# RWKV-7 time mixer on one core: when the triangular solve and the block inverses are done, and which engine forms the keys' factors

## The chip, the cores and the metric

The kernel runs on one core of a Trainium2 chip. Its engines run side by side, each with its own queue in program order: TensorE (PE, matrix products, with PEld for its weight loads), VectorE (DVE), ScalarE (ACT), GpSimd (POOL) and SyncE (SP), which here only issues DMAs. The metric is the time of one launch in microseconds of the device; the median of three runs of the kernel before is 1370.06 us (1367.29 to 1370.53).

## The reference

A two-layer encoder trunk, 512 tokens, 1024 channels, float32. Layer 0 mixes tokens with RWKV-7, layer 1 with latent attention; each layer also has a ConvFFN with gated GELU. The change touches the RWKV-7 mixer alone:

```
def _rwkv7_step(S, inp):
    r, w, k, v, a, b = inp
    sa = einsum('bhvk,bhk->bhv', S, a)
    S = S * w[:, :, None, :] + sa[..., None] * b[:, :, None, :] + v[..., None] * k[:, :, None, :]
    return S, einsum('bhvk,bhk->bhv', S, r)

def rwkv7_time_mix(x, ...):
    xs = x + (x_prev - x) * mu                    # six mixtures
    r, k, v = (xs[i] @ w_rkv[i] for i in range(3))
    w_log = -softplus(-(w0 + tanh(xw @ w1) @ w2)) - 0.5
    decay = exp(-exp(w_log))
    a = sigmoid(a0 + (xa @ a1) @ a2)
    g = sigmoid(xg @ g1) @ g2
    kk = normalize(k * k_k)                       # per head of 64 channels
    k = k * (1.0 + (a - 1.0) * k_a)
    y = scan(_rwkv7_step, zeros, (r, decay, k, v, -kk, kk * a))
    yn = groupnorm(y) * lnx_w + lnx_b
    bonus = sum(r * k * r_k) * v
    return ((yn + bonus) * g) @ w_o
```

## The kernel before, in words

**Tiling.** Channels lie on partitions, in 8 tiles `p` of 128 (two heads each); tokens lie in the free dimension, 512 of them. The recurrence is done in 8 chunks of 64 tokens: within a chunk, the term `a` makes a triangular system of 64 by 64 for each of the 16 heads, which is inverted; across chunks a state `S` of 64 by 64 a head is carried. Matrix products with weights are three passes of a shorter float32 format (`mm3`, L131 to L133); for that each weight tile is split into a high part by ScalarE (`whi`) and a rest by VectorE (`wlo`, L125).

**Stages of `time_mix`.** First the projections, in three groups: keys, values, receptances. While TensorE runs the values' projection, the *key tiles* are formed, interleaved by `keyed`: `factors(p)` makes the decay factors (`ar[..., 0, :]` holds exponentials shifted by one token, `ar[..., 1, :]` unshifted ones, `en` their inverse), `ka` = `a * k_a + (1 - k_a)`, and the squares `ksq`; `key2(p)` sums these on TensorE (`ps_kn`), makes the reciprocal root `krv` and finishes both halves of `ar` and `bk`; `ab(p)` multiplies the two for the triangular systems and writes them to DRAM (`s_ab`) with DMAs that GpSimd issues. `recept(p)` then multiplies the receptances in, takes the decay at each chunk's end (`pc`), and makes `rkk` for the bonus; `bonus(p)` sums that on TensorE (`ps_bo`).

**The solve.** `solve()` is a generator of 2 times 31 steps on VectorE, each two `tensor_tensor` (into `tm`, then onto the matrix, both L85; in the rows the solve's tiles are `s` or `s_1562`). Its first half inverts the 32 by 32 diagonal blocks of chunks 0 to 3, its second half those of chunks 4 to 7. At a half's end GpSimd writes the result out (`s_xd`), ScalarE copies a transposed half, and GpSimd writes that too (`s_x1`). Only then, for the second half, ScalarE copies the next matrix in (`sA`), and a memset and ones are laid down.
`steps(n)` issues n steps at a place of the program: two with each input tile of the receptances' first three output tiles (18), then per tile from the table at L698, then per chunk from the table at the chunk loop.

**The inverses.** `fetch_x(ch)` reads a chunk's blocks back from DRAM (nine kinds of pieces, on SyncE's queue), into `TB[ch % 2]`, `LT` and `X1`. `inv1` (matmuls `ps_i1`, then a copy `wi`) and `inv2` (`ps_i2`, copied into `TB`) complete the 64 by 64 inverses. The kernel before does chunk 0's and chunk 1's before the chunk loop and then, in chunk `ch`, those of `ch + 2`.

**The chunk loop.** A chunk does `u_step` (`ps_u` from `v` and `lu`), half of the next chunk's scores (`ps_sc`, masked by VectorE into `lu` and `m`), `u2_step` (`ps_u` from `TB` and `u`), the other scores, state product (`s_step`), token transposes (`ps_tk`), outputs and the transposes of the chunk before. The output's gates (`gate(p, hf)`: four matmuls of 256 columns for 8 tiles, and for each half of the tokens) lie in chunks 0 and 4: in chunk 0 four tiles ahead of `u2_step` and four at the chunk's end.

**What sets the order.** A list scheduler orders the instructions of each engine, by program order and by offsets of priority: weights are brought forward (by 70, and 160 in `proj`), steps of the solve not (`SP = 0`). What is ready early is put early, so an instruction can stand well before its place in the program, but each engine then runs its queue strictly in that order: an instruction that waits holds all behind it.

Of the kernel before, what the change touches and what calls it, by code (L numbers as in the profile page):

```python
# [48 lines left out]
def c3(ap):  # L49
    return ap.rearrange("q (c t) -> q c t", t=C)  # L50
# [6 lines left out]
class Trunk:  # L57
# [243 lines left out]
    def time_mix(self, nxt, cp, gt):  # L301
# [8 lines left out]
        ap = self.open("apool")  # L310
        ar = ap.tile([P, DT, NCH, 2, C], F32, name="ar")
        bk = ap.tile([P, DT, NCH, 2, C], F32, name="bk")
# [5 lines left out]
        lw = self.open("lw", side="right")  # L318
        scan = t1.tile([P, T], F32, name="scan")
        w1 = lw.tile([P, D], F32, tag="w1", name="w1")  # L320
        g1 = [lw.tile([P, n], F32, tag=f"g{i}", name="g1") for i, n in enumerate((512, 768))]
        g1k = lambda o, n: g1[0][:, o:o + n] if o < 512 else g1[1][:, o - 512:o - 512 + n]
        x = self.x
# [112 lines left out]
        qk = group(1, 0, first, prio=G0)  # L436
        for t, n in ((w1, I["w1"]), (g1[0], I["g1"][:, :512]), (g1[1], I["g1"][:, 512:]), (self.cst, I["cst"][:, :256]), (self.ident, I["cst"][:, 256:]), (scan, I["scan"])):
            nc.sync.dma_start(out=t, in_=n)
# [61 lines left out]
        for p in range(5, DT):  # L500
            kept(p, qk[p - 5])
        nc.gpsimd.memset(ar[:, :, :, 0, 0:1], 1.0)
        self.use_log_exp()

        def factors(p):
            cp = cs[:, p, :]
            self.act(ar[:, p, :, 0, 1:C], c3(cp)[:, :, 0:C - 1], AF.Exp, scale=-CD)
            en = t1.tile([P, T], F32, tag="en", name="en")
            self.act(en, cp, AF.Exp, scale=CD)
            ka = t1.tile([P, T], F32, tag="ka", name="ka")  # L510
            self.act(c3(ka), bk[:, p, :, 0, :], AF.Identity, scale=V("ka", p), bias=om[:, 48 + p:49 + p])
            self.act(ar[:, p, :, 1, :], c3(cp), AF.Exp, scale=-CD)
            self.tt(ka, ka, en, ALU.mult)
            self.tt(bk[:, p, :, 0, :], bk[:, p, :, 0, :], c3(en), ALU.mult)
            kr = tp.tile([P, T], F32, tag="kr", name="kr", bufs=3)
            self.act(c3(kr), bk[:, p, :, 1, :], AF.Copy, scale=V("kk", p))
            sq = tp.tile([P, T], F32, tag="sq", name="ksq", bufs=3)
            self.act(c3(sq), bk[:, p, :, 1, :], AF.Square, scale=V("kk", p))
            self.tt(bk[:, p, :, 1, :], bk[:, p, :, 1, :], c3(ka), ALU.mult)
            return p, kr, sq  # L520

        def key2(p, kr, sq):
            pn = bank2("ps_kn")
            mm(pn, lhsT=self.bones, rhs=sq, start=True, stop=True)
            rv = tp.tile([P, T], F32, tag="sq", name="krv", bufs=3)
            self.act(rv, pn, AF.Ln, bias=self.tiny)
            self.act(rv, rv, AF.Exp, scale=-0.5)
            self.stt(kr, rv, 1e12, kr, ALU.min, ALU.mult)
            self.tt(ar[:, p, :, 0, :], c3(kr), ar[:, p, :, 0, :], ALU.mult)
            self.tt(bk[:, p, :, 0, :], c3(kr), bk[:, p, :, 0, :], ALU.mult)  # L530
# [144 lines left out]
        def recept(p, q):  # L675
            nc.vector.tensor_copy(out=self.pc[:, :, p], in_=ar[:, p, :, 1, C - 1])
            self.tt(ar[:, p, :, 1, :], c3(q), ar[:, p, :, 1, :], ALU.mult)
# [16 lines left out]
        for p in range(DT):  # L694
            q = qr[p] if p < 3 else proj(0, p)
            if len(rp) == BL:
                bonus(*rp.pop(0))
            steps((0, 0, 0, 7, 7, 3, 3, 3)[p])  # L698
            rp.append(recept(p, q))
            if p in (5, 7):  # L700
                fetch_x(p // 2 - 2)
                w = inv1(p // 2 - 2, bank2)
            if p == 6:
                inv2(0, w, bank2)
        def score_mm(ch, g):
# [7 lines left out]
        while rp:  # L713
            bonus(*rp.pop(0))
        inv2(1, w, bank2)
        gate_weights()
# [20 lines left out]
        WU.append(buf("u"))  # L737
        self.sign = s1.tile([P, 1], F32, name="sign")
        nc.vector.tensor_copy(out=self.sign, in_=self.mincl[:, C - 1:C])
        M, LU, VS, S, YC, ends = {}, {}, {}, {}, {}, {}  # L740
# [123 lines left out]
        for ch in range(NCH):  # L864
            n = ch + 1
            u = u_step(ch)
            if n < NCH:
                scores(n, (0,))
            if ch == 0:
                for p in range(4):  # L870
                    gate(p, 0)
            u2_step(ch, u)
            if n + 1 < NCH:
                fetch_x(n + 1)
            if n < NCH:
# [6 lines left out]
            if ch < 3:  # L882
                steps((11, 12, 1)[ch])
            y_tokens(ch, q)
            if ch > 0:
                yt(ch - 1)
            if ch in (0, 4):
                for p in range(0 if ch else 4, DT):
                    gate(p, ch // 4)
            if n + 1 < NCH:  # L890
                fetch_v(n + 1)
                w = inv1(n + 1)
            if 5 <= ch:
                fill(2)
            if n + 1 < NCH:
                inv2(n + 1, w)
            if ch == 6:
# [420 lines left out]
```

## Time and profile before

| | |
|---|---|
| median of three runs | 1370.06 us |
| the profiled execution, its own time | 1370.63 us |
| its span | 1368.9 us |
| granted TensorE clock, mean over the span | 0.975 |
| PE busy | 1307.6 us, 96% (8108 instructions) |
| PEld busy | 1077.8 us, 79% |
| DVE busy | 815.6 us, 60% |
| ACT busy | 708.8 us, 52% |
| POOL busy | 291.8 us, 21% |
| moved by DMA | 141.41 MB, 103 GB/s on average |

The span is that of the recorded instructions; the execution's own time is 1.7 us more. The busy times are sums over the whole program. A granted clock of 1 is TensorE's higher level (2.4 GHz), 0.5 its lower one (1.2 GHz); a number between is a mean over the stretch. In a row of the trace the first number is the start in us from the span's beginning, the second the duration, and a bracket at the end gives the time that the engine stood idle before the row and what released it.

### The profile page before, as it was taken

How to read it: one execution, taken by the hardware profiler on the slowest of the kernel's cores; microseconds unless marked ns; L12 is line 12 of the kernel's file. 1: busy time of each engine (PE TensorE's matmuls, PEld its weight loads, DVE VectorE, ACT ScalarE, POOL GpSimd, SP SyncE). 2: the span in 40 equal slices, each digit the busy share in tenths (PEclk: the TensorE clock that was granted, in tenths of full speed). 3: DMA queues.
4: the chain of work that ended last, by engine and by line, in shares of the span. 5: the costliest groups of instructions: out<-in, count | busy, mean ns of one | idle time of the engine just before them, and what ended most of it. 6: DMA issues, size and time to landing. Idle time of an engine off the chain costs nothing.

```text
span 1368.9 us, 21882 instructions
## 1 busy us (share of the span) xinstructions
PE 1307.6 (96%) x8108; PEld 1077.8 (79%) x8108; DVE 815.6 (60%) x1512; ACT 708.8 (52%) x1353; POOL 291.8 (21%) x277
## 2 busy tenths in 40 slices
PE   7989997989999999999999999999999999999995
PEld 5467775878998888888888877777898888888885
DVE  7668787677797666665233887873566555541003
ACT  6699842567676444444232566674464444433231
POOL 0001421100010000000000241222355444444443
PEclk9999998899999999999999999999999999999998
DMA  6121593345533323223333145441223222233321
GB/s 208 61 77 63 169 260 90 77 106 132 170 124 124 100 94 100 98 95 92 94 98 94 44 119 116 106 106 47 78 77 101 100 93 100 99 90 93 97 77 62
DMA packets 111211, 141.41 MB, mean 103 GB/s; under 512 B 47552, under 2 KB 54592, under 8 KB 111104
## 3 DMA queue, kind: packets, MB, share of 16 engines
q1 hardware_dynamic: 107696, 129.52, 32.2%
q0 software_dynamic: 3408, 10.49, 2.4%
q8 instruction: 64, 1.05, 0.3%
q14 instruction: 43, 0.35, 0.1%
HBM read 120.31 MB, written 12.58 MB: 97 GB/s over the span
## 4 chain that ended last, share of the span: by engine, by line
PE 75%; DVE 11%; ACT 7%; issue 3%; DMA 2%; POOL 1%; SPq 0%; POOLq 0%; ACTq 0%; DVEq 0%
PE ps_in L132 11%; PE ps_in L133 11%; PE ps_in L131 11%; PE ps_out L131 7%; PE ps_out L133 7%; PE ps_out L132 7%; PE ps_pj L132 1%; PE ps_pj L131 1%; PE ps_pj L133 1%; PE ps_o L1185 1%; DVE wlo L125 1%; DVE x L220 1%; PE ps_sc L710 1%; PE ps_t L1169 1%; ACT whi L82 1%
## 5 line engine op out<-in xcount | busy, mean ns | idle before, releaser
L82 ACT ACTIVATE whi<-wraw 128x512 fp32r<-128x512 f32 (+2 forms) x411 | 249.6, 614 | 356.9 <-PE ps_out L133 132.9
L132 PE MATMUL ps_in<-xl,whi 128*128 128x512 f32 (+1 forms) x768 | 286.9, 374 | 4.8 <-DVE xl L88 4.8
L131 PE MATMUL ps_in<-xh,wlo 128*128 128x512 f32 (+1 forms) x768 | 286.8, 374 | 0.8 <-DVE wlo L125 0.7
L125 POOL TENSOR_TENSOR wlo<-wraw,whi 128x512 fp32r<-128x512 f32 (+2 forms) x176 | 221.8, 1266 | 304.4 <-ACT whi L82 299.0
L133 PE MATMUL ps_in<-xh,whi 128*128 128x512 f32 (+1 forms) x768 | 285.7, 373 | 0.0
L125 DVE TENSOR_TENSOR wlo<-wraw,whi 128x512 fp32r<-128x512 f32 x229 | 154.0, 679 | 92.7 <-ACT whi L82 90.8
L132 PEld LDWEIGHTS ps_in<-xl,whi 128*128 128x128 f32 x768 | 145.5, 190 | 31.3 <-DVE xl L88 6.3
L131 PEld LDWEIGHTS ps_in<-xh,wlo 128*128 128x128 f32 x768 | 145.3, 190 | 26.7 <-DVE wlo L125 0.9
L133 PEld LDWEIGHTS ps_in<-xh,whi 128*128 128x128 f32 x768 | 145.6, 190 | 24.8
L131 PE MATMUL ps_out<-hh,wlo 128*128 128x512 f32 (+1 forms) x396 | 146.6, 370 | 1.3 <-ACT mg L82 1.3
L133 PE MATMUL ps_out<-hh,whi 128*128 128x512 f32 (+1 forms) x396 | 145.3, 367 | 0.0
L132 PE MATMUL ps_out<-hl,whi 128*128 128x512 f32 (+1 forms) x396 | 144.1, 364 | 0.0
L85 DVE TENSOR_TENSOR macc<-macc,msq 128x512 f32<-128x512 f32 (+1 forms) x25 | 15.5, 619 | 136.1 <-ACT msq L82 136.1
L237 POOL TENSOR_TENSOR row<-row,msq 128x256 f32<-128x256 f32 x14 | 14.1, 1010 | 379.8 <-ACT msq L82 379.3
L131 PE MATMUL ps_pj<-xh,wlo 128*128 128x512 f32 x192 | 79.0, 430 | 8.6 <-ACT xh L82 6.7
L88 DVE SCALAR_TENSOR_TENSOR c<-gp,vec,c 128x512 f32<-128x512 f32 x88 | 72.6, 827 | 24.1 <-ACT c L82 22.7
L131 PEld LDWEIGHTS ps_out<-hh,wlo 128*128 128x128 f32 x396 | 74.4, 188 | 13.5 <-ACT mg L82 1.9
L133 PEld LDWEIGHTS ps_out<-hh,whi 128*128 128x128 f32 x396 | 74.3, 188 | 13.5
L132 PEld LDWEIGHTS ps_out<-hl,whi 128*128 128x128 f32 x396 | 74.3, 188 | 13.1
L132 PE MATMUL ps_pj<-xl,whi 128*128 128x512 f32 x192 | 77.2, 404 | 0.3 <-DVE xl L85 0.2
L133 PE MATMUL ps_pj<-xh,whi 128*128 128x512 f32 x192 | 76.5, 400 | 0.0
L85 DVE TENSOR_TENSOR u<-ps_in,row 128x512 f32<-128x512 f32 x44 | 30.3, 689 | 63.0 <-PE ps_in L133 63.0
(289 smaller groups left out, 2385.2 us busy)
## 6 DMA issues: line engine op xcount, KB each, us to landing
wraw<-in_win SPq DMA_DIRECT2D x176, 256.0 KB, 2.7
wraw<-in_wout SPq DMA_DIRECT2D x80, 256.0 KB, 2.6
wraw<-in_wrkv SPq DMA_DIRECT2D x48, 256.0 KB, 3.2
wraw<-in_wo SPq DMA_DIRECT2D x32, 256.0 KB, 2.9
x<-in_xT SPq DMA_DIRECT2D x16, 256.0 KB, 4.7
wraw<-in_ow SPq DMA_DIRECT2D x16, 256.0 KB, 3.1
s_ab<-ab POOLq DMA_DIRECT2D x16, 128.0 KB, 2.8
s_vt<-vT POOLq DMA_DIRECT2D x8, 256.0 KB, 2.8
```

Source lines behind the costliest of these rows:

```text
L82: self.nc.scalar.activation(out=out, in_=in_, func=func, **kw)
L85: self.nc.vector.tensor_tensor(out=out, in0=a, in1=b, op=op)
L88: self.nc.vector.scalar_tensor_tensor(out=out, in0=a, scalar=s, in1=b, op0=op0, op1=op1)
L125: self.wlo.tensor_tensor(out=l[:, :w], in0=r, in1=h[:, :w].bitcast(F32), op=ALU.subtract)
L131: mm(ps, lhsT=wl, rhs=xh, start=start, stop=False)
L132: mm(ps, lhsT=wh, rhs=xl, start=False, stop=False)
L133: mm(ps, lhsT=wh, rhs=xh, start=False, stop=stop)
L220: eng.tensor_tensor(out=xk, in0=xk, in1=mg, op=ALU.add)
L237: (self.nc.gpsimd if (h, k) in ACCP else self.nc.vector).tensor_tensor(out=self.acc2[:, c], in0=self.acc2[:, c], in1=sq, op=ALU.add)
L710: mm(qs[hd][:, p], lhsT=b, rhs=a, start=True, stop=True)
L1169: nc.tensor.transpose(out=q[:, o:o + P], in_=pr[i][:, j * P:(j + 1) * P], identity=t.ident)
L1185: nc.tensor.matmul(q[HALF[i], j * P:], lhsT=VT[pr // 4][j][:, c:c + 64], rhs=w, start=j == 0, stop=j == QB - 1)
```

## The change

Key tiles: the shifted exponential (8 of ScalarE's) is dropped. `before(p)` reads the unshifted one with an offset of one token, after a memset of 1.0 on VectorE in the last column of each chunk. For this `ar` becomes a view of a larger tile `art`, and `w1`, `g1` and `scan`, which are used before `ar` is written, are laid into it (with one DMA for `g1` instead of two). The keys' bias form `ka` goes from ScalarE to VectorE, the copy `pc` from VectorE to ScalarE.

Solve and inverses: the solve's steps come after `recept` in the loop over tiles, with the table (0, 0, 0, 5, 5, 4, 0, 0), which is 32 steps ahead of the chunk loop with the 18 of the first three tiles; the rest lies in the chunks. Chunk 0's blocks are fetched after the projections, and its inverse is done among the gates of chunk 0, now all eight of them ahead of `u2_step`. From there on chunk `ch` does the inverse of `ch + 1`. `sign` is a view instead of a copy.

```diff
-        ar = ap.tile([P, DT, NCH, 2, C], F32, name="ar")
+        art = ap.tile([P, DT * NCH * 2 * C + P], F32, name="ar")
+        ar = art[:, :DT * NCH * 2 * C].rearrange("q (p c s t) -> q p c s t", p=DT, c=NCH, s=2)
...
-        nc.gpsimd.memset(ar[:, :, :, 0, 0:1], 1.0)
+        def before(p):
+            nc.vector.memset(ar[:, p, :, 0, C - 1:C], 1.0)
+            o = p * NCH * 2 * C + C - 1
+            return art[:, o:o + NCH * 2 * C].rearrange("q (c s t) -> q c s t", s=2, t=C)[:, :, 0, :]
         def factors(p):
             cp = cs[:, p, :]
-            self.act(ar[:, p, :, 0, 1:C], c3(cp)[:, :, 0:C - 1], AF.Exp, scale=-CD)
...
-            self.act(c3(ka), bk[:, p, :, 0, :], AF.Identity, scale=V("ka", p), bias=om[:, 48 + p:49 + p])
+            nc.vector.tensor_scalar(out=c3(ka), in0=bk[:, p, :, 0, :], scalar1=V("ka", p), scalar2=om[:, 48 + p:49 + p], op0=ALU.mult, op1=ALU.add)
...
-            self.tt(ar[:, p, :, 0, :], c3(kr), ar[:, p, :, 0, :], ALU.mult)
+            self.tt(ar[:, p, :, 0, :], c3(kr), before(p), ALU.mult)
...
         def recept(p, q):
-            nc.vector.tensor_copy(out=self.pc[:, :, p], in_=ar[:, p, :, 1, C - 1])
+            self.act(self.pc[:, :, p], ar[:, p, :, 1, C - 1])
...
-            steps((0, 0, 0, 7, 7, 3, 3, 3)[p])
             rp.append(recept(p, q))
-            if p in (5, 7):
-                fetch_x(p // 2 - 2)
-                w = inv1(p // 2 - 2, bank2)
-            if p == 6:
-                inv2(0, w, bank2)
+            steps((0, 0, 0, 5, 5, 4, 0, 0)[p])
+        fetch_x(0)
...
-        inv2(1, w, bank2)
...
             if ch == 0:
+                w = inv1(0)
                 for p in range(4):
                     gate(p, 0)
+                inv2(0, w)
+                for p in range(4, DT):
+                    gate(p, 0)
+                fetch_x(1)
             u2_step(ch, u)
-            if n + 1 < NCH:
-                fetch_x(n + 1)
...
-                steps((11, 12, 1)[ch])
+                steps((11, 11, 40)[ch])
...
-            if ch in (0, 4):
-                for p in range(0 if ch else 4, DT):
-                    gate(p, ch // 4)
+            if ch == 4:
+                for p in range(DT):
+                    gate(p, 1)
+            if n < NCH:
+                w = inv1(n)
             if n + 1 < NCH:
                 fetch_v(n + 1)
-                w = inv1(n + 1)
             if 5 <= ch:
                 fill(2)
+            if n < NCH:
+                inv2(n, w)
             if n + 1 < NCH:
-                inv2(n + 1, w)
+                fetch_x(n + 1)
```

On TensorE, from the last projection to the first chunk's masks, the order before; `ps_i_2021` and `ps_i_2087` are the two parts of chunk 0's inverse, `ps_i_2166` and `ps_i_2200` those of chunk 1's, `ps_bo` the bonus sums (tiles 4 to 7 are left here) and `ps_sc` scores.

```order
L133 MATMUL ps_pj<-xh,whi 128x512
L710 MATMUL ps_sc<-ar,bk 128x128 x8
L659 MATMUL ps_i_2021<-s_1562 64x64 x8
L686 MATMUL ps_bo<-rkk,cst 128x512
L668 MATMUL ps_i_2087<-wi,s_1562 64x64 x8
L686 MATMUL ps_bo<-rkk,cst 128x512
L659 MATMUL ps_i_2166<-T_1793,s_1562 64x64 x8
L686 MATMUL ps_bo<-rkk,cst 128x512 x2
L710 MATMUL ps_sc<-ar,bk 128x128 x2
L668 MATMUL ps_i_2200<-wi,s_1562 64x64
```

The same place of TensorE's queue after the change, up to the first `ps_u` (`ps_tk` are token transposes).

```order
L133 MATMUL ps_pj<-xh,whi 128x512
L690 MATMUL ps_bo<-rkk,cst 128x512
L711 MATMUL ps_sc<-ar,bk 128x128 x8
L690 MATMUL ps_bo<-rkk,cst 128x512 x2
L711 MATMUL ps_sc<-ar,bk 128x128 x8
L769 MATMUL ps_tk<-ident,bk 128x64 x16
L777 MATMUL ps_u<-v,lu_2172 64x64
```

And the start of chunk 0's inverse after the change (`ps_i_2261`), behind the first `ps_u`, with the first gate's four matmuls (`ps_g`).

```order
L777 MATMUL ps_u<-v,lu_2173 64x64
L663 MATMUL ps_i_2261<-s_1556 64x64 x8
L131 MATMUL ps_g<-gt,wlo 128x256
L132 MATMUL ps_g<-gxl,whi 128x256
L133 MATMUL ps_g<-gt,whi 128x256
L558 MATMUL ps_g<-gt,whi 128x256
```

Both inverses have left the stretch between the projections and the first `ps_u`, chunk 0's to behind that `ps_u` and chunk 1's to the end of chunk 0; one bonus sum has moved ahead of the scores.

On VectorE, at the end of the solve's first half, the order before: the last step (128x31), a receptance product (`ar<-ps_pj,ar`), then the memset and the second half's first steps.

```order
L85 TENSOR_TENSOR tm<-s_1562 128x31
L85 TENSOR_TENSOR s_1562<-s_1562,tm 128x31
L85 TENSOR_TENSOR ar<-ps_pj,ar 128x8x64
L612 MEMSET s_1562 128x32
L85 TENSOR_TENSOR tm<-s_1562 128x31
L85 TENSOR_TENSOR s_1562<-s_1562,tm 128x31
```

The same place after the change (`vTr` is a bonus product, `rkk` what a bonus sum waits for).

```order
L85 TENSOR_TENSOR tm<-s_1556 128x31
L85 TENSOR_TENSOR s_1556<-s_1556,tm 128x31
L85 TENSOR_TENSOR ar<-ps_pj,ar 128x8x64
L85 TENSOR_TENSOR vTr<-ps_bo,vTr 128x512
L85 TENSOR_TENSOR whi<-wraw,whi 32x512
L88 SCALAR_TENSOR_TENSOR rkk<-ar,vec,bk 128x512
L616 MEMSET s_1556 128x32
L85 TENSOR_TENSOR tm<-s_1556 128x31
L85 TENSOR_TENSOR s_1556<-s_1556,tm 128x31
L85 TENSOR_TENSOR ar<-ps_pj,ar 128x8x64
L85 TENSOR_TENSOR vTr<-ps_bo,vTr 128x512
L88 SCALAR_TENSOR_TENSOR rkk<-ar,vec,bk 128x512
```

The receptance product behind the first half's last step is the last tile's before and the seventh tile's after the change; the last tile's, and with it `rkk` of the last bonus, now stands behind the memset and one step of the second half. Of the second half ten steps stood here before the masks, now one.

## Rows read from the trace of the kernel before

**Rows 1.** Windows: us, busy us by engine with instructions, granted clock, DMA share, GB/s

```profile
100.00:110.00 10.00, 7.02 (x22) 4.84 (x22) 6.77 (x12) 10.00 (x18) 0.00 (x0) 0.83 0.08 25
140.00:150.00 10.00, 7.79 (x52) 5.11 (x51) 6.84 (x13) 9.04 (x18) 5.44 (x7) 0.85 0.48 150
210.00:220.00 10.00, 10.00 (x44) 7.94 (x43) 9.36 (x25) 3.22 (x5) 2.09 (x4) 1.00 0.38 111
230.00:240.00 10.00, 5.90 (x44) 3.18 (x46) 7.21 (x22) 1.92 (x6) 1.02 (x2) 0.54 0.23 36
250.00:260.00 10.00, 10.00 (x90) 8.91 (x86) 4.92 (x12) 3.15 (x7) 0.00 (x0) 0.52 0.11 25
260.00:270.00 10.00, 9.90 (x190) 9.04 (x192) 8.50 (x20) 7.21 (x19) 0.00 (x0) 1.00 0.38 77
```

**Rows 2.** Timeline of TensorE: bonus, scores, inverse, both ps_u, gates

```profile
200.18 1.02 PE L686 MATMUL ps_bo<-rkk,cst 128*128 128x512 f32 x2
...
224.68 1.16 PE L710 MATMUL ps_sc<-ar,bk 64*128 64x128 f32 x16
234.10 1.12 PE L659 MATMUL ps_i<-s 128*64 128x64 f32 x16 [8.26 <-DMA s<-s_x]
...
249.70 1.11 PE L778 MATMUL ps_u<-v,lu 64*64 64x64 f32 x14
...
258.18 1.79 PE L787 MATMUL ps_u<-u,s 128*64 128x64 f32 x32
...
264.75 0.28 PE L133 MATMUL ps_g<-gt,whi 128*128 128x256 f32 x1
264.87 0.28 PE L554 MATMUL ps_g<-gt,whi 96*128 96x256 f32 x1
...
268.43 0.80 PE L778 MATMUL ps_u<-v,lu 128*64 128x64 f32 x18
...
270.32 1.15 PE L787 MATMUL ps_u<-u,T 128*64 128x64 f32 x32
```

**Rows 3.** Timeline of VectorE: a key product, both solve halves' edge, two mask products

```profile
157.59 0.68 DVE L85 TENSOR_TENSOR bk<-kr,bk 128x512 f32<-128x512 f32 x1
...
222.87 0.21 DVE L85 TENSOR_TENSOR s<-s,tm 128x31 f32<-128x31 f32 x1
...
229.63 0.19 DVE L85 TENSOR_TENSOR tm<-s 128x31 f32<-128x31 f32 x1 [1.86 <-ACT s L82]
...
261.10 0.43 DVE L85 TENSOR_TENSOR lu<-ps_sc,cst 64x256 f32<-64x256 f32 x1 [1.48 <-PE ps_sc L710]
261.54 0.42 DVE L85 TENSOR_TENSOR m<-ps_sc,cst 128x256 f32<-128x256 f32 x1
```

**Rows 4.** Timeline of ScalarE: the second half's matrix is copied

```profile
228.54 1.06 ACT L82 ACTIVATE s<-s 128x1024 f32<-128x1024 f32 x1 [3.28 <-DMA s_x<-s]
```

**Rows 5.** Key tiles: tiles (min/median/max ns, starts), timeline; by form (us, mean)

```profile
L82 ACT ACTIVATE ar<-cs x16: 606/616/642, 78.9 to 143.2; 128x504 f32<-128x504 f32 x8, 128x512 f32<-128x512 f32 x8
...
L676 DVE COPY pc<-ar x8: 167/170/1005, 102.4 to 143.8; 128x8 f32<-128x8 f32 x8
...
100.38 0.80 ACT L82 ACTIVATE ka<-bk,om,vec 128x512 f32<-128x512 f32 x1
...
102.98 2.08 PE L524 MATMUL ps_kn<-ksq,cst 128*128 128x512 f32 x2 [3.65 <-ACT ksq L82]
...
143.83 1.00 DVE L676 COPY pc<-ar 128x8 f32<-128x8 f32 x1 [1.40 <-ACT ar L82]
143.85 0.95 POOL L611 MEMSET s<- 128x1024 f32 x1 [0.68 <-ACT ar L82]
...
146.01 1.14 PE L524 MATMUL ps_kn<-ksq,cst 128*128 128x512 f32 x2 [2.21 <-ACT krv L82]
...
L1159 DVE TENSOR_SCALAR p<-p,mx 128x512 f32<-128x512 f32 x16 | 8.3, 517 | 0.3
```

**Rows 6.** Timeline of TensorE: the inverse of chunk 4

```profile
293.03 0.69 PE L659 MATMUL ps_i<-s 128*64 128x64 f32 x16 [1.55 <-issue]
```

More of the change, by code (lines that the diff above doesn't have):

```diff
@@ L318, in time_mix @@
         lw = self.open("lw", side="right")
[L319 to L322, printed above, removed]
+        scan = art[:, 7 * D:7 * D + T]
+        w1, g1 = art[:, 3 * D:4 * D], art[:, 4 * D:4 * D + 1280]
+        g1k = lambda o, n: g1[:, o:o + n]
         x = self.x
@@ L436, in time_mix @@
         qk = group(1, 0, first, prio=G0)
-        for t, n in ((w1, I["w1"]), (g1[0], I["g1"][:, :512]), (g1[1], I["g1"][:, 512:]), (self.cst, I["cst"][:, :256]), (self.ident, I["cst"][:, 256:]), (scan, I["scan"])):
+        for t, n in ((w1, I["w1"]), (g1, I["g1"]), (self.cst, I["cst"][:, :256]), (self.ident, I["cst"][:, 256:]), (scan, I["scan"])):
             nc.sync.dma_start(out=t, in_=n)
@@ L737, in time_mix @@
         WU.append(buf("u"))
-        self.sign = s1.tile([P, 1], F32, name="sign")
-        nc.vector.tensor_copy(out=self.sign, in_=self.mincl[:, C - 1:C])
+        self.sign = self.mincl[:, C - 1:C]
         M, LU, VS, S, YC, ends = {}, {}, {}, {}, {}, {}
```

## The prediction

> **What bounds the kernel now.** I read the views in this order: busy time by engine and slice, ten-microsecond windows over the first layer's time mixer, TensorE's order of time where a window shows it idle, then VectorE, ScalarE and GpSimd at the same place. The part of the program that the change touches ends before 360 us; after that TensorE's slices are at 9 throughout, and I expect the same time there. In the windows [rows 1] TensorE works 10 of 10 us almost everywhere, with two kinds of exception. The large one is between the projections and the chunk loop: 5.90 us busy in 230:240, and a granted clock of 0.54 there and of 0.52 in 250:260, that is mostly the lower level, 1.2 GHz. The small ones are 100:110 (7.02 busy, clock 0.83) and 140:150 (7.79, 0.85).
>
> The large hole begins when the last projection ends: the first chunk's scores start at 224.68, and then TensorE waits 8.26 us for the DMAs that bring the solved blocks of chunk 0 (`ps_i`, 234.10) [rows 2]. What it waits for is a chain that begins on VectorE: the last step of the triangular solve's first half ends at 222.87 + 0.21 = 223.08 [rows 3]; ScalarE transposes a copy, GpSimd writes it out, and ScalarE copies the second half's matrix only when that write has left its buffer (228.54, after 3.28 us of idle time) [rows 4], and VectorE's first step of the second half starts at 229.63 [rows 3]. So from the solve's end it is 11.0 us to the inverse on TensorE and 6.55 us to VectorE's next step. The clock is lost with the wait: chunk 0's `ps_u` of 32 matmuls takes 1.79 us at 258.18 and chunk 1's 1.15 us at 270.32 [rows 2].
>
> **The change, term 1: the hole.** Before, from the scores (224.68) to chunk 0's second `ps_u` (258.18) it is 33.5 us. I work out the same stretch for the new order, from T, the place of those scores. One more bonus sum (two matmuls, 1.0 us [rows 2]) now stands ahead of them, as two of the six that are done by then moved up; call T' = T + 1.0.
>
> The solve's first half keeps its 31 steps between the same kinds of work on VectorE, but it begins two weight subtractions earlier and ends before the seventh receptance product instead of behind it. Before, it ended 1.6 us ahead of the scores. The engine is full there (9.36 of 10 us in 210:220 [rows 1]), so I don't count the scheduler's whole lead: 2.8 us ahead of T', bounds 0 and 6. The blocks of chunk 0 are then there at T' - 2.8 + 11.0 = T' + 8.2.
>
> VectorE now has a wait in its queue. The memset and step 0 of the second half stand ahead of the last receptance product, the last bonus product and all eight mask products, and they come at T' - 2.8 + 6.55 = T' + 3.8. Behind it step 0 (0.4), then three 128x512 operations of about 0.65 (such a row lasts 0.68 [rows 3] and overlaps the next a little): T' + 6.1. TensorE meanwhile does one bonus (1.0), scores (1.1), one bonus, and waits from T' + 3.1 to 6.1 for the last bonus; with that, the other scores and the token transposes it is at T' + 9.1. VectorE finishes the bonus product and eight mask products of 0.44 apart [rows 3] at T' + 10.8, and the first `ps_u` ends at about T' + 11.5. The blocks (T' + 8.2) are there, so the 8.26 us are gone, and what is late next is VectorE's queue, 3 us.
>
> Then inverse, first part (0.65), 16 gate matmuls, inverse, second part (0.7), 16 gate matmuls. Gate matmuls follow each other at 0.12 us at the high level [rows 2], so 1.9 for 16: T' + 16.7 = T + 17.7. At the lower level this last piece of 5.2 us is up to twice as long; I take half of that, 2.6, since the engine idles 3 us and works thinly before. T + 20.3, so 13.2 less than 33.5. The gates of tiles 4 to 7 no longer follow in chunk 0 (1.9 saved), the inverse of chunk 1 does (1.3 paid). Term 1: -13.8, call it -14. Bounds: -19 with the full lead and the high level, -8 with no lead, the lower level all the way and a bonus more.
>
> **Term 2: the tiles of keys (98 to 160 us).** Of ScalarE's 16 exponentials on `cs` for `ar`, 8 of 0.62 us go, and 8 bias forms of 0.80 [rows 5]; 11.3 us of busy time in a stretch where ScalarE has no gap. It gets 8 copies of 8 columns; no such copy stands there, so between 0.17 (VectorE's [rows 5]) and 0.6 (a whole tile) each: 2.4 at 0.3. VectorE loses those 8 copies (0.17 each, one 1.00) and gets 8 two-scalar operations on 128x512, nearest row 0.52 [rows 5], between 0.3 and 0.75, and 8 memsets of 8 columns under 0.2: +4 us, most of it hidden, as VectorE is busy 6.77 and 6.84 of 10 us in the two windows [rows 1].
>
> What TensorE gains is only what it waited: 3.65 us at 102.98 for the first `ksq` and 2.21 us at 146.01 for a `krv` [rows 5], and what the clock costs behind each, 1.7 and 1.5 us (10 us less 0.83 and 0.85 of them [rows 1]). The first wait shortens by the 1.2 us of bias form and exponential that stood between table load and `ksq` (0.80 and 0.62 [rows 5], less 0.1 of overlap each). The second one hangs on a buffer whose write-out is under way, so I give it half of nothing to 3.9: -2. Against it +1 for subtractions that VectorE now does later. Term 2: -2, bounds -9 and +5.
>
> **Term 3: the chunks.** The second half's steps 1 to 9 move from the hole into chunks 0 to 2; with them the solve ends in chunk 2, not 1, and its copy on ScalarE and the short wait of chunk 4's inverse (1.55 us at 293.03 [rows 6]) move to chunk 3. Steps on VectorE stand ahead of mask products and states in program order. In chunk 0 they run under the gates; behind it 7, 6 and 6 steps are left from one state product to the next, where 10 and 6 were. At 0.4 a step (its two operations took 0.19 and 0.21 [rows 3]; wider ones more) that is some 3 us of a chunk of 12 (258.18 to 270.32 [rows 2]), so no chunk carries more than before, and one more carries some: +0.5, bounds 0 and +4. Four weight DMAs of 256 KB now stand ahead of chunk 4's blocks on the sync queue, but while the queue would wait for the solve anyway.
>
> The inverses one chunk ahead rather than two cost nothing by themselves: their blocks are fetched at a chunk's end and wanted a whole chunk later, where before they had two thirds of one. The placement of `w1`, `g1` and `scan` in `ar`, one DMA instead of two for `g1`, and `sign` without its copy are under 0.3 us together, hidden by full engines.
>
> **Sum.** -14 - 2 + 0.5 = -15.5 from the profiled execution's 1370.63 (span 1368.9): 1355.1. That execution is 0.57 above the median of the three runs, 1370.06, so against it 1354.6.
>
> **Rivals.** *1. VectorE's queue stays late.* The engine is as good as full up to the solve's end; every microsecond that this end slips holds the last bonus, the masks and the first `ps_u` alike. With an end 5 us behind T' - 2.8 the wait is 8 us, as long as the old one, and the clock is lost as before: -7 instead of -14, 1361.6, and with the chunks' bound 1365. For it: before, the half ended 1.6 us ahead of the scores, and nothing on VectorE was taken out of this stretch. Against it: one product less stands ahead of that end.
>
> *2. VectorE becomes the bound of the key tiles.* Then term 2 is +5: 1361.6. For it is one row: the copy `pc` at 143.83 took 1.00 us instead of 0.17, from GpSimd's memset at 143.85 to that one's end [rows 5]; eight operations that met GpSimd so would cost up to 8 us of VectorE. Against it: seven of eight copies met nothing.
> The Trainium skill has a rule behind that row ("SBUF — State Buffer", section "Who interferes with whom"): GpSimd and a VectorE instruction in a two-port mode, which a `tensor_scalar` can enter and a `tensor_tensor` can't, lock each other out for a whole instruction. The trace agrees with its 1.00 us. By the rule the change puts eight more such instructions where GpSimd issues the `s_ab` writes, whose delay would hold the solve too; without the rule term 2 would lie nearer -4.
>
> *3. Slower.* The clock doesn't come back. Place: chunks 0 to 3, whose matmuls are of 64 columns with waits between; all wide gate matmuls now lie before them. Price: at the lower level 14 such matmuls took 1.11 us (249.70), at the higher 18 took 0.80 (268.43) [rows 2], 1.8 times as long each; about 10 us of them in a chunk, less 2 of waits that it covers, is +6, and over four chunks +24: 1378.6. It decides if TensorE is still at 1.2 GHz when chunk 1 begins. For it: clock 0.52 in 250:260 though TensorE was busy all 10 us. Against: 1.00 in 260:270 with the same small matmuls.
> The Trainium skill says that the low level is the default and that activity releases it ("TensorE: Matmul & The Clock Gate", Part 1); the windows agree (0.54 in the hole), and by it a thin loop behind an idle engine is the place to look.
>
> *4. More.* The key tiles give back both waits and the clock behind them (-9), the hole 16: 1345.
>
> **Chances.** The forecast's own case 0.66 (1348 to 1361), rival 1 0.12, rival 2 0.08, rival 3 0.04, rival 4 0.10. Range 1343 to 1366: it takes rivals 1, 2 and 4 in for the most part and leaves out rival 3 and the tails. Under 0.3% (4.1 us) a measurement of this kernel can't tell from no change. Rivals 1 and 2 together, or either with the chunks' bound, reach there: 0.07. Slower is rival 3 and a little of the tails, 0.05. Faster 0.88.
>
> **What would show it.** Right: no wait of TensorE for `s_x` or `s_xd` at the first inverse; the scores-to-second-`ps_u` stretch 17 to 24 us instead of 33.5; a wait of 2 to 4 us for `rkk` at the last bonus; the first `ksq` wait near 2.4. Wrong: a wait for blocks at any inverse of over 2 us, a clock under 0.9 in chunks 1 to 3, VectorE rows of the bias form over 0.8, or a first stage that ends later than before.

## The result and the profile after

The changed kernel takes 1352.91 us (median of 4 runs, 1350.07 to 1355.32) against 1368.67 us for the kernel before beside it: 0.9888, 95% interval 0.9856 to 0.9921. The forecast was 1354.6 us. A later measurement of the same kernel (after_again) gave 0.9872 (0.9848 to 0.9895).

The profiled execution took 1355.32 us with a span of 1353.6 us, 15.3 less than before. I cut both spans at the same three places: the first chunk's scores without the bonus sum that now stands ahead of them (T in the forecast), the second `ps_u` of chunk 0, and that of chunk 7.

| stretch | before | after | difference | forecast |
|---|---|---|---|---|
| start to T (key tiles, projections) | 224.68 | 224.66 | 0.0 | -2 |
| T to chunk 0's second `ps_u` | 33.50 | 14.91 | -18.6 | |
| to chunk 7's second `ps_u` | 98.50 | 101.84 | +3.3 | |
| the rest | 1012.2 | 1012.2 | 0.0 | 0 |

In the forecast's own division 0.6 us of the chunks (gates gone, one inverse more) belongs to term 1. So term 1 is -19.2 where -14 stood (its bound was -19), term 2 is 0.0 for -2, and term 3 is +3.9 for +0.5. The sum is right, and each term is off.

The timeline of TensorE in the changed kernel, answering to [rows 2]:

```profile
224.66 1.02 PE L690 MATMUL ps_bo<-rkk,cst 128*128 128x512 f32 x2
225.61 1.16 PE L711 MATMUL ps_sc<-ar,bk 64*128 64x128 f32 x16
226.71 1.99 PE L690 MATMUL ps_bo<-rkk,cst 128*128 128x512 f32 x4
...
234.14 0.69 PE L663 MATMUL ps_i<-s 128*64 128x64 f32 x16
...
236.86 0.68 PE L672 MATMUL ps_i<-wi,s 64*64 64x64 f32 x16
...
239.57 1.15 PE L786 MATMUL ps_u<-u,s 128*64 128x64 f32 x32
```

No row has a bracket: TensorE waits neither for the blocks (8.26 us before) nor for the last bonus (3 us in the forecast). The second `ps_u` of 32 matmuls takes 1.15 us and no longer 1.79. VectorE's timeline shows why nothing waits (to [rows 3]):

```profile
178.78 0.18 DVE L85 TENSOR_TENSOR tm<-s 128x31 f32<-128x31 f32 x1
...
218.33 0.21 DVE L85 TENSOR_TENSOR s<-s,tm 128x31 f32<-128x31 f32 x1
...
223.76 0.09 DVE L616 MEMSET s<- 128x32 f32 x1 [1.01 <-POOL s L615]
225.18 0.19 DVE L85 TENSOR_TENSOR tm<-s 128x31 f32<-128x31 f32 x1 [1.33 <-ACT s L82]
...
226.71 0.74 DVE L88 SCALAR_TENSOR_TENSOR rkk<-ar,vec,bk 128x512 f32<-128x512 f32 x1
```

The solve's first half ends at 218.54, 7.07 us ahead of the scores. The forecast took 2.8, with 0 and 6 as bounds. The wait in VectorE's queue that it described is there, 1.33 us in front of the second half's first step at 225.18, and 6.64 us after the first half's end (6.55 before). But it comes before TensorE needs what stands behind it. The first step lies at 178.78. It needs the key tiles' products, which GpSimd writes to `s_ab` and SyncE's queue (SPq) reads back. In the kernel before, the last write, the last of these reads and the same step stood here (timelines of GpSimd, SyncE's queue and VectorE, kernel before):

```profile
167.44 1.49 POOL L541 DMA_DIRECT2D s_ab<-ab  x2 [2.37 <-ACT ab L82]
...
173.03 4.12 SPq L597 DMA_DIRECT2D s<-s_ab  x1
...
184.08 0.18 DVE L85 TENSOR_TENSOR tm<-s 128x31 f32<-128x31 f32 x1
```

and in the changed kernel the last write and the last read, and the rows that answer to [rows 5] (TensorE's waits, and by tile the bias form and the copy; those two with min/median/max ns and first and last start):

```profile
102.40 1.23 PE L528 MATMUL ps_kn<-ksq,cst 128*128 128x512 f32 x2 [2.43 <-ACT ksq L82]
...
154.66 1.97 PE L541 MATMUL ps_ab<-ar,bk 64*64 64x64 f32 x32 [2.16 <-ACT krv L82]
...
164.14 1.49 POOL L545 DMA_DIRECT2D s_ab<-ab  x2 [2.15 <-ACT ab L82]
...
172.99 0.59 SPq L601 DMA_DIRECT2D s<-s_ab  x1
...
L515 DVE TENSOR_SCALAR ka<-bk,vec,om x8: 529/542/547, 83.4 to 148.7; 128x512 f32<-128x512 f32 x8
...
L82 ACT ACTIVATE pc<-ar x8: 202/204/209, 139.2 to 140.6; 128x8 f32<-128x8 f32 x8
```

The key tiles end 3.3 us sooner (164.14 against 167.44), and the solve starts 5.3 us sooner. The last read starts at the same time in both, but took 4.12 us to issue and landed 9.0 us after its start before, 0.59 and 4.8 after. Why it was slow before is not shown. TensorE itself gains nothing here in this execution: its first wait fell by 1.2 us as worked out, but the second is as long as before, 8.7 us later and at another place (`ps_ab` for `ps_kn`). The windows (columns as in [rows 1]):

```profile
100.00:110.00 10.00, 7.60 (x23) 5.43 (x24) 8.64 (x15) 9.99 (x18) 0.00 (x0) 0.83 0.10 32
150.00:160.00 10.00, 7.84 (x81) 5.61 (x80) 6.79 (x12) 6.92 (x12) 3.73 (x5) 0.83 0.35 97
220.00:230.00 10.00, 10.00 (x69) 6.97 (x69) 5.74 (x13) 4.86 (x7) 4.86 (x8) 1.00 0.68 179
230.00:240.00 10.00, 10.00 (x139) 8.89 (x138) 8.06 (x24) 6.90 (x19) 1.69 (x4) 1.00 0.50 111
270.00:280.00 10.00, 8.56 (x154) 7.46 (x154) 8.68 (x25) 7.45 (x15) 0.57 (x1) 0.83 0.57 166
280.00:290.00 10.00, 7.12 (x146) 6.32 (x142) 7.56 (x14) 7.05 (x14) 0.53 (x1) 0.88 0.52 132
```

The old hole (220 to 240) is closed at a clock of 1.00. From chunk 2's second `ps_u` to chunk 4's it is 29.22 us for 26.91 before, so the loop loses 2.3 us around chunk 4's inverse, to [rows 6] (timelines of VectorE, GpSimd, SyncE's queue and TensorE):

```profile
278.09 0.20 DVE L85 TENSOR_TENSOR s<-s,tm 128x31 f32<-128x31 f32 x1
...
278.82 0.57 POOL L623 DMA_DIRECT2D s_xd<-s  x1 [47.13 <-issue]
...
282.72 0.82 SPq L653 DMA_DIRECT2D s<-s_xd  x2
...
287.41 0.99 PE L663 MATMUL ps_i<-s 128*64 128x64 f32 x16 [2.09 <-DMA s<-s_xd]
```

The solve's second half ends 6.1 us sooner than before (278.29 against 284.38). The loop runs 18.6 us sooner, but the inverse stands a chunk later in it, so TensorE wants these blocks at 285.32 for 291.48, 6.2 us sooner. The wait is nearly that of before: 9.12 us from the last step to the inverse and 2.09 of waiting, for 8.65 and 1.55. (The trace names no releaser for the 1.55 us; they end 2.4 us after the start of the last read of these blocks, at 290.59.) What is new is the lower clock around it. The forty us that hold this inverse, in the kernel before, in the changed kernel and in sq4, one of the runs below:

```profile
262.00:302.00 40.00, 35.00 (x762) 31.16 (x759) 33.60 (x79) 26.96 (x58) 1.10 (x2) 1.00 0.37 83
262.00:302.00 40.00, 35.45 (x692) 32.05 (x691) 31.39 (x70) 27.43 (x55) 1.10 (x2) 0.91 0.41 101
262.00:302.00 40.00, 34.12 (x706) 30.63 (x708) 31.94 (x68) 28.85 (x62) 1.10 (x2) 1.00 0.47 119
```

In sq4, with the same waits within 0.4 us (2.28 at the inverse) and a clock of 1.00, the two chunks take 27.33 us, 0.4 more than before. The rest of the 2.3 us is the clock. The last interval, from chunk 6's second `ps_u` to chunk 7's, takes 2.0 us more (16.66 for 14.62): 1.3 is the inverse that now stands in it, and 0.56 a wait of chunk 7's second `ps_u` for `u`. The first two chunks give 1.2 back, since 1.9 us of gates are gone from them.

### The profile page after: what moved, and what is told of

Read it like the earlier page. It is cut to its first block, busy times and chain, and to the rows that moved or that the text cites. A ratio compares the mean times of both kernels' runs of the same rounds, so it can differ in the third digit from the quotient of the medians.

```text
span 1353.6 us, 21896 instructions
## 1 busy us (share of the span) xinstructions
PE 1300.0 (96%) x8108; PEld 1072.7 (79%) x8108; DVE 816.5 (60%) x1519; ACT 701.3 (52%) x1345; POOL 291.5 (22%) x276
## 4 chain that ended last, share of the span: by engine, by line
PE 67%; DVE 8%; ACT 3%; DMA 2%; issue 1%; POOL 1%; SPq 0%; POOLq 0%; DVEq 0%; ACTq 0%
PE ps_in L132 11%; PE ps_in L133 11%; PE ps_in L131 11%; PE ps_out L131 7%; PE ps_out L133 7%; PE ps_out L132 7%; PE ps_o L1190 1%; DVE x L220 1%; PE ps_t L1174 1%; PE ps_wo L131 1%; PE ps_s L131 1%; PE ps_wo L133 1%; PE ps_wo L132 1%; DVE xl L88 1%; PE ps_s L132 1%
```

## The experiments

A table of what the traces of all runs show, in us: T' is the start of the first chunk's scores; lead is from the end of the solve's first half to T'; hole is from T' to chunk 0's second `ps_u`; loop from there to chunk 7's. Ratios are to the kernel before on the same chip, with 95% intervals. (In before and keys_only no bonus sum stands directly ahead of T'.) The times come from one trace each, and places move between executions of one kernel: the changed kernel's first step is at 178.78 in one trace and at 175.98 in the other (after_again), T' with it. The lead is 7.07 in both, so the runs are compared by it.

| kernel | ratio (interval) | first step | T' | lead | hole | loop |
|---|---|---|---|---|---|---|
| before | 1 | 184.08 | 224.68 | 1.60 | 33.50 | 98.50 |
| changed | 0.9888 (0.9856 to 0.9921) | 178.78 | 225.61 | 7.07 | 13.96 | 101.84 |
| keys_only | 0.9965 (0.9947 to 0.9983) | 178.69 | 223.11 | 5.30 | 30.20 | 97.91 |
| order_only | 0.9929 (0.9906 to 0.9952) | 183.75 | 226.13 | 2.34 | 19.92 | 99.72 |
| ka_back | 0.9924 (0.9899 to 0.9950) | 184.86 | 226.83 | 1.84 | 18.08 | 99.71 |
| exp_back | 0.9906 (0.9881 to 0.9931) | 182.56 | 225.53 | 2.65 | 18.84 | 99.63 |
| steps_early | 0.9894 (0.9867 to 0.9922) | 178.84 | 225.66 | 7.07 | 13.96 | 102.12 |
| sq4 | 0.9868 (0.9840 to 0.9897) | 175.66 | 222.87 | 7.84 | 13.96 | 100.31 |
| sq4_fetch | 0.9882 (0.9856 to 0.9908) | 175.02 | 222.22 | 7.85 | 13.96 | 100.49 |
| sq4_fetch_steps | 0.9909 (0.9886 to 0.9932) | 173.87 | 221.13 | 7.85 | 13.96 | 102.27 |
| after_again | 0.9872 (0.9848 to 0.9895) | 175.98 | 223.59 | 7.07 | 13.96 | 102.03 |
| sq4_again | 0.9869 (0.9844 to 0.9894) | 177.48 | 224.72 | 7.84 | 13.96 | 101.01 |
| sq4_fetch_again | 0.9868 (0.9842 to 0.9893) | 178.33 | 225.60 | 7.85 | 13.96 | 102.50 |

**keys_only: the key tiles' edits with the solve and inverses as before.** The hunks of the order are undone, such as:

```diff
+            steps((0, 0, 0, 7, 7, 3, 3, 3)[p])
             rp.append(recept(p, q))
-            steps((0, 0, 0, 5, 5, 4, 0, 0)[p])
```

> Only the key-tile edits (shifted exponential dropped, bias form on VectorE, pc on ScalarE); solve steps and inverses stand as before the change. Theory 1 (the edits pay through the solve): TensorE's first stage is as long as before (last projection near 224), but the solve's first step comes near 179 us instead of 184.1, its first half ends near 218.5 instead of 223.1, and the wait for chunk 0's blocks falls from 8.3 to 3 or 4 us; total 4 to 7 us under the kernel before. Theory 2 (the forecast's term: only TensorE's waits in the key tiles count): total -2 us, the first half ends at 222 to 223 and the wait for the blocks stays near 8.

Measured: 1365.22 us, -4.7 by the medians. The order is that of before, yet the first half ends 5.3 us sooner and the wait for the blocks falls from 8.26 to 4.50 us (VectorE, then TensorE, in keys_only; the first row is the solve's first step, which starts as soon as the read of `s_ab` has landed):

```profile
178.69 0.19 DVE L85 TENSOR_TENSOR tm<-s 128x31 f32<-128x31 f32 x1 [1.22 <-DMA s<-s_ab]
...
217.59 0.22 DVE L85 TENSOR_TENSOR s<-s,tm 128x31 f32<-128x31 f32 x1
...
228.77 0.89 PE L663 MATMUL ps_i<-s 128*64 128x64 f32 x16 [4.50 <-DMA s<-s_x]
```

Theory 1 holds in its place: 3.3 us of the gain are in the hole. T' is 1.6 us sooner too, which theory 1 had not; that is the forecast's own term.

**order_only: the new order with the key tiles as before.** The edit is the change without its hunks for `ar`, `factors`, `before`, `ka` and `pc`, and without those for `sign` and for the places of `w1`, `g1` and `scan`.

> Only the new order of the solve's steps and of the inverses; key tiles as in the kernel before. Theory 1 (the solve starts late without the key edits): first step near 184, first half ends near 222 to 223, the last bonus waits for rkk 2 to 4 us on TensorE as the forecast had it, total -9 to -13 us. Theory 2 (the order of the steps alone brings the solve's end forward): first half ends near 218.5, no wait for rkk, total -14 to -17 us.

Measured: 1360.68 us, -9.3. With the -4.7 of keys_only that is -14.0, for -15.8 with both. The lead is 2.34, the hole 19.9 us against 19.3 by the forecast's sum. VectorE and the windows in order_only:

```profile
223.57 0.22 DVE L85 TENSOR_TENSOR s<-s,tm 128x31 f32<-128x31 f32 x1
...
230.05 0.09 DVE L612 MEMSET s<- 128x32 f32 x1 [2.46 <-POOL s L611]
```

```profile
230.00:240.00 10.00, 8.42 (x87) 7.01 (x84) 8.28 (x25) 5.14 (x9) 3.93 (x7) 0.64 0.53 120
240.00:250.00 10.00, 10.00 (x135) 9.28 (x137) 8.09 (x22) 5.32 (x15) 0.00 (x0) 0.85 0.28 52
```

Theory 1 has the first step and the total right; the first half's end, 223.79, is 0.8 beyond its 222 to 223. One detail is wrong: `rkk` of the last bonus stands ahead of the memset here, so no bonus waits for it. The memset's 2.46 us hold the bonus products and masks instead. TensorE's waits up to the second `ps_u` come to only 1.6 us, and the clock falls to 0.64.

**ka_back and exp_back: one edit of the key tiles undone in the changed kernel.** For ka_back:

```diff
-            nc.vector.tensor_scalar(out=c3(ka), in0=bk[:, p, :, 0, :], scalar1=V("ka", p), scalar2=om[:, 48 + p:49 + p], op0=ALU.mult, op1=ALU.add)
+            self.act(c3(ka), bk[:, p, :, 0, :], AF.Identity, scale=V("ka", p), bias=om[:, 48 + p:49 + p])
```

> The changed kernel with the keys' bias form back on ScalarE (the exponential still dropped, pc still on ScalarE). Theory 1 (ScalarE's work in the key tiles sets when the solve starts): 8 activations of 0.80 us come back on a full engine; the solve's first step moves from 178.8 to between 181 and 183, its first half's end with it, the lead of 7.1 us over the scores shrinks to 3 to 5, total +1 to +3 us against the changed kernel. Theory 2 (VectorE's share matters as much, the bias form costs it 0.54 each): first step stays at 178 to 180, total within 1 us.

For exp_back `factors` makes the shifted exponential again (`self.act(ar[:, p, :, 0, 1:C], ...)`), and `before(p)` returns `ar[:, p, :, 0, :]`.

> The changed kernel with the shifted exponential back on ScalarE (bias form still on VectorE). Theory 1 (ScalarE sets the solve's start): 8 exponentials of 0.61 us come back; first step between 181 and 182, total +1 to +2.5 us. Theory 2: first step stays at 178 to 180, total within 1 us.

Measured: first step at 184.86 and 182.56, leads of 1.84 and 2.65, holes 4 to 5 us longer than in the changed kernel. A row of VectorE in ka_back, the copy that stands ahead of the solve and waits for the read of `s_ab`:

```profile
182.67 1.08 DVE L606 COPY s<-s 128x1024 f32<-128x1024 f32 x1 [3.64 <-DMA s<-s_ab]
```

The leads lie beyond theory 1's bounds in the direction that it named, and theory 2 is out: either activation back on ScalarE is enough to lose most of the lead. The last write to `s_ab` is at 167.71 and 167.02 with them, as late as before (167.44), and the last read lands 9 to 10 us after its start again. Why half of the relief gives less than half of the lead is not shown. Their loops are 2.1 us shorter than the changed kernel's: 1.6 to 1.7 us between the second `ps_u` of chunks 2 and 4, where no inverse waits for blocks, and 1.2 from chunk 0's to chunk 1's. In the totals (1358.13 and 1354.19 us) exp_back's interval overlaps that of the changed kernel measured beside it (after_again, 0.9848 to 0.9895), and ka_back's lies just above; behind the loop the rest took 1007.6 us in ka_back's profiled execution and 1012.2 in the changed kernel's, at a granted clock of 0.99 and 0.98, so a total carries some us of chance.

**steps_early: the loop's loss.**

```diff
-                steps((11, 11, 40)[ch])
+                steps((11, 40, 0)[ch])
```

> The changed kernel with the solve's rest issued in chunk 1 (chunk table 11, 40, 0 instead of 11, 11, 40). Theory 1 (the chunks lose 3 to 4 us to the late end of the solve's second half): the end comes some 3 to 4 us sooner, the 2.09 us wait of chunk 4's inverse for s_xd goes, the granted clock of 0.83 and 0.88 around it returns to 1.00, total 2 to 4 us under the changed kernel, about 1350. Theory 2 (VectorE's queue is what holds the chunks): the steps delay the masks of chunks 2 and 3, new waits of 1 to 2 us there, total equal to the changed kernel or up to 2 us more.

Measured: the loop is 102.1 us, and the total is not better. Timelines of TensorE and VectorE in steps_early:

```profile
272.65 0.33 PE L777 MATMUL ps_u<-v,lu 128*64 128x64 f32 x2 [2.34 <-ACT v L82]
...
276.03 0.20 DVE L85 TENSOR_TENSOR s<-s,tm 128x31 f32<-128x31 f32 x1
...
287.52 0.69 PE L663 MATMUL ps_i<-s 128*64 128x64 f32 x16 [2.15 <-DMA s<-s_xd]
```

The solve ends 2.1 us sooner, yet the inverse waits as long. SyncE's queue in steps_early shows why:

```profile
279.70 0.82 SPq L653 DMA_DIRECT2D s<-s_xd  x2
284.11 0.78 SPq L656 DMA_DIRECT2D s<-s_x  x2
284.94 0.92 SPq L653 DMA_DIRECT2D s<-s_xd  x2
```

The second head's diagonal blocks (284.94) stand behind reads of `s_x`, which is written later. And the steps hold VectorE's states: ScalarE waits 2.94 us for them to make `v`, and `ps_u` waits 2.34 for `v` where it waited 0.93. Theory 2 holds.

**sq4: four buffers.** All six tiles of the tag `sq` get `bufs=4` for `bufs=3`.

> The changed kernel with four buffers instead of three for the tiles that hold ksq, krv and ab. Theory 1 (a buffer still being written out holds krv): ScalarE's 2.09 us wait at 150 us for the s_ab write goes, TensorE's 2.16 us wait at 154.7 and the clock of 0.83 in 150:160 with it, total 2 to 4 us under the changed kernel. Theory 2 (VectorE and ScalarE are full in this stretch): the wait moves to another key tile and the total stays within 1 us.

Measured: 1351.88 us. The wait moves: ScalarE no longer waits for the `s_ab` write, but TensorE waits for VectorE's `bk`, 1.32 us in this run and 2.92 in the next of the same kernel. The runs further down decide for theory 2.

**sq4_fetch and sq4_fetch_steps: both heads' diagonal and lower blocks are read ahead of `s_x`.** In `fetch_x`:

```diff
                 nc.sync.dma_start(out=LT[o + 32:o + 64, :, n], in_=lov[g, c, hd])
+            for hd in range(2):
+                o, n = hd * 64, slice(hd * 32, hd * 32 + 32)
                 for i in range(2):
```

> Four buffers as in the run sq4, and fetch_x reads the diagonal blocks and lower blocks of both heads before the pieces of s_x, which only the inverse's second part needs. Theory 1 (the second head's diagonal blocks stand on SyncE's queue behind reads that wait for the later write of s_x): the 2.28 us wait of chunk 4's inverse falls to about 1.5, since the s_xd write itself lands only 4 us after the solve's end; total 0 to 1 us under sq4. Theory 2 (the wait is set by the write of s_xd alone): no change of the wait.

> As sq4_fetch, and the solve's rest is issued in chunk 1 (chunk table 11, 40, 0). Theory 1 (end of the solve and order of the reads together make the wait): chunk 4's inverse waits under 0.5 us, total 2 to 3 us under sq4, about 1349. Theory 2 (the steps cost at the masks of chunks 2 and 3 what the wait gives, as in steps_early, where ps_u waited 2.34 us): total as sq4 or up to 2 us more.

Measured: chunk 4's inverse waits 0.70 us in sq4_fetch, 1.82 in a second trace of the same kernel (sq4_fetch_again), and not at all with the early steps. From the solve's end to the inverse it is 7.7 and 8.8 us with the new order of the reads, and 9.1 to 10.2 in four traces with the old one, so the order gives something over 1 us. How much the end of the solve gives is not shown: with the early steps the loop itself comes to the inverse over 2 us later. And with the early steps the 2.34 us wait of `ps_u` stays, and the clock behind it was 0.50 from 272 to 276. Theory 2 has the total of sq4_fetch_steps: no gain.

**Three kernels side by side.** after_again is the changed kernel itself.

> The changed kernel once more, on the same chip as sq4_again and sq4_fetch_again. Both theories of sq4: 0.987 to 0.990 of the kernel before, as measured first (0.9888).

> Four buffers for ksq, krv and ab. Theory 1 (the wait at 150 to 155 us and the clock behind it are really gone): 2 to 4 us under after_again beside it, and the windows from 148 to 160 at a granted clock of 1.00. Theory 2: within 1 us of after_again; the first difference was one of chips and of chance in the clock.

> Four buffers and the reads of both heads' diagonal blocks first. Theory 1 (chunk 4's inverse waits 0.7 instead of 2.1 us and the clock holds more often): 1 to 2 us under sq4_again. Theory 2 (the clock falls or holds in chunks 2 and 3 by chance): within 1 us of sq4_again.

Measured: 1353.44, 1352.99 and 1353.00 us. Theory 2 for both: no version found here beats the changed kernel by what can be measured. after_again shows the share of chance in term 2: same code, T' 2.0 us sooner than in the first profile. Of this, 0.7 us is there at 77 us already, ahead of the key tiles. Then there is a wait of 2.00 us at 154.10 in place of 2.16, with this window in place of 0.83 (after_again):

```profile
154.10 1.15 PE L541 MATMUL ps_ab<-ar,bk 64*64 64x64 f32 x32 [2.00 <-ACT krv L82]
...
191.59 1.10 PE L690 MATMUL ps_bo<-rkk,cst 128*128 128x512 f32 x2 [0.46 <-DVE rkk L88]
```

```profile
150.00:160.00 10.00, 8.00 (x87) 5.73 (x85) 8.40 (x14) 8.45 (x16) 5.23 (x7) 1.00 0.35 91
```

From `ps_ab` to the next wait it is 37.49 us here and 38.94 in the first profile, whose next wait is this one:

```profile
193.60 1.10 PE L690 MATMUL ps_bo<-rkk,cst 128*128 128x512 f32 x2 [0.45 <-DVE rkk L88]
```

So the lower clock behind this wait cost 1.45 us.

## Why the prediction was right, and which of its steps were not

- **What bounds the kernel, and the mechanism of the hole: right.** The wait for the blocks is gone, the clock in 220 to 240 is 1.00, and nothing changed behind the time mixer (1012.2 us both times; 1007.6 to 1012.5 over all traces).
- **The sum for the hole: right in size for what it assumed, not in its parts.** At the lead that it took, 2.8 us, it gives 19.3 us from T'. The three runs with leads of 1.84 to 2.65 have 18.1 to 19.9. But it had 3 us of waiting for `rkk` and 2.6 of clock in it. In none of the three does a bonus wait for `rkk`; of the 4.1, 4.9 and 6.0 us above 13.96 TensorE's waits make 0.7, 1.6 and 1.6 (ka_back, exp_back, order_only), and the rest goes with the lower clock (0.75, 0.79 and 0.64 in 230:240, 0.91, 0.87 and 0.85 in 240:250). That the sizes agree is partly luck. At 7.07 us and over it is 13.96 us in all eight traces, since no wait is left.
- **The step that failed: "2.8 us ahead of T', bounds 0 and 6".** I had the solve begin two weight subtractions earlier by the new order on VectorE (about 1.2 us), and nothing earlier by the data that it needs. (The subtractions move with the key tiles' edits, too: keys_only has them behind the step, order_only ahead of it as before.) Its first step needs the reads of `s_ab`, which follow the key tiles, so term 2 feeds term 1. The lead is 7.07 us, beyond the bound of 6. The stretch from the scores to the second `ps_u` fell to 14.0 us, below the 17 to 24 that I named. keys_only shows the cause: 5.3 us at the first half's end without the new order of solve and inverses; ka_back and exp_back lose it again with one activation. The relief of ScalarE was costed only by TensorE's own waits, which was the small part.
- **Term 2: -2, measured 0.0, -1.6 and -2.0** (changed, keys_only, after_again). The size is right in two of the three, not the reason. Counted from a wait at 77 to 78 us, ahead of the key tiles, the three are -0.7, -1.8 and -2.0. The first wait's 1.2 us came in all of them. The second wait, to which -2 was given, didn't shorten (2.16, 2.23 and 2.00 us for 2.21), and 1.45 us between the two traces of the changed kernel is the clock behind it. The 1.7 us that the forecast put on the clock behind the first wait is no cost: the last section has it.
- **Term 3: +0.5, measured +3.9, at the bound.** I counted steps per chunk and found none fuller than before, and I took the short wait of chunk 4's inverse over into chunk 3. It did move there, 0.5 us longer; what I put at nothing is the clock around it. The clock of 0.83 and 0.88 could cost up to 10 x 0.17 + 10 x 0.12 = 2.9, an estimate; of the loop's loss 2.3 us lie there, wait and clock together. Some 0.7 us more lie in the first two chunks and 0.9 in the last two. So the inverses one chunk ahead did cost something. Two signs named as "wrong" in the forecast came: a wait over 2 us at an inverse, and a clock under 0.9 in chunks 1 to 3. Of the signs named as "right", the first `ksq` wait came at 2.43, and the wait for `rkk` came in no run.
- **The total was right in part by luck:** the hole gave 5.2 us more than forecast, the key tiles and the chunks 2 and 3.4 less.
- **Rivals.** 1 (VectorE's queue late) showed in no run: with one activation back the holes are 18 to 19 us, the forecast's own case. 2 fell: all eight bias forms took 529 to 547 ns, none was lengthened. But only one of them, at 128.35, met an instruction of GpSimd (a DMA issue), so the lock-out was hardly put to the test. 3 fell in chunks 0 and 1 (1.00 from 220 to 270), and showed for some us in chunks 2 and 3. 4 came by half: the hole gave 19.2 us, more than its 16, and the key tiles 0 to 2 where it had 9.

## What to carry to other kernels

When an engine is relieved, follow its results to the next stage's start before counting only who waits for it now: a stage whose own time hardly changes can still hand over 5 us sooner. When a chain is pulled ahead, compare the new ends of all producers with the new start of each consumer; here the solve's second half and the inverse that wants it both moved 6 us, and the short wait between them stayed. Price the clock around such a wait from rows at both levels, and not the wait alone. And judge gains of 1 or 2 us behind short waits from several executions.

## What the hardware showed that I had not expected

sq4_fetch and sq4_fetch_again are one kernel. In both traces TensorE waits for the first `ksq`, 2.42 and 2.43 us, and these are the windows behind it, of sq4_fetch

```profile
100.00:110.00 10.00, 8.30 (x29) 5.18 (x30) 9.79 (x17) 9.52 (x18) 0.00 (x0) 1.00 0.02 7
```

and of sq4_fetch_again:

```profile
100.00:110.00 10.00, 7.76 (x24) 5.58 (x25) 8.80 (x15) 9.99 (x18) 0.00 (x0) 0.83 0.10 31
```

A difference of 3.4 us in T' (222.22 and 225.60) looks like the price of this clock, and most of it is not. From `ps_kn` to TensorE's next wait, of sq4_fetch

```profile
100.91 1.12 PE L528 MATMUL ps_kn<-ksq,cst 128*128 128x512 f32 x2 [2.42 <-ACT ksq L82]
...
111.27 0.50 PE L131 MATMUL ps_pj<-xh,wlo 128*128 128x512 f32 x1 [0.54 <-DVE wlo L125]
```

and of sq4_fetch_again:

```profile
102.23 1.13 PE L528 MATMUL ps_kn<-ksq,cst 128*128 128x512 f32 x2 [2.43 <-ACT ksq L82]
...
112.59 0.50 PE L131 MATMUL ps_pj<-xh,wlo 128*128 128x512 f32 x1 [0.52 <-DVE wlo L125]
```

Both take 10.36 us: at the higher clock TensorE waited for its inputs instead (0.27 and 0.48 us for `xh` and `xl`). The 1.3 us between the two traces were there ahead of this wait. It is behind the second wait (1.84 and 2.37 us, at 151.75 and 153.62) that the clock counts: 1.00 against 0.83 in 150:160, and 1.5 us more up to the next wait.

So a wait of about 2 us was followed by the higher clock in one execution and by the lower one in another, at 100 and at 150 us alike, and what that costs is read from the next common place and not from the window's clock. The clock also fell behind shorter waits: in the changed kernel after 0.93, 0.32 and 0.18 us (271.70 to 273.11), where the next 18 `ps_u` took 1.22 us. In sq4 the same three waits (0.93, 0.33, 0.18) were followed by 0.80. Executions of the changed kernel spread over 5 us (1350.07 to 1355.32). How much of that comes from these waits is not shown, for the part behind the loop varied as well (1007.6 to 1012.5 us).
